# A hybrid pooling and attention block on one Trainium2 core: pooling's running sums moved from DMAs to VectorE, attention's halves added in DRAM while the attention still runs

## The chip, the cores and the metric

The kernel runs on one core of one Trainium2 chip, in one launch. The metric is the device time of that launch in microseconds (us); smaller is better. The core has TensorE (PE) for matrix products, VectorE (DVE), ScalarE (ACT), GpSimd (POOL) and SyncE (SP). SP, ACT and POOL can each put DMAs on their queue; DMAs that add to their destination are issued by POOL in this kernel. Everything is float32. Products run in "float32r" with each operand split into a high part and a low remainder, and three passes (high by high, high by low, low by high) are added.

## The reference, cut to what matters

One decoder layer on x of 1024 positions by 1024 channels:

```python
h = rmsnorm(x, g_mix_pre)
u_pool, q, k, v, gates = split(h @ w_in + b_in)
# pooling: 4 groups of 128 channels, windows 2, 4, 8, 16 along the sequence
pooled[g][t] = (cs[t] - cs[t - w]) / min(t + 1, w)          # a running mean, cs = cumsum(u_pool)
y_pool = ((pooled - u_pool) @ w_pool[g]) * pool_scale
# attention: 8 query heads on 2 key/value heads, window 128, with a sink logit per head
y_attn = softmax_with_sink(rotary(q) @ rotary(k).T) @ v
merged = sigmoid(gate_p) * (y_pool @ w_branch_pool) + sigmoid(gate_a) * (y_attn @ w_branch_attn)
x = x + rmsnorm(merged @ w_out, g_mix_post)
x = x + rmsnorm(square(relu(rmsnorm(x) @ w_up)) @ w_down, g_mlp_post)
```

A window that is a power of two can be summed by doubling: a sum over 2 is t[i] + t[i-1], a sum over 4 is that result plus itself shifted by 2, and so on. Windows 2, 4, 8 and 16 take 1, 2, 3 and 4 such steps, ten in all.

## The kernel before, in words

Activations lie with channels on the 128 partitions and the 1024 positions in the free dimension, except in the attention, where positions lie on partitions. Products with large weights (gates and pooling input, output projection, up and down projection) use a seven-product scheme: the class `Pairs` (L471) takes weight tiles in pairs and needs the products 1 to 7 of each pair, `gt.mm(bank, p, i)` at L544 being one of them (12 matmuls). Pairs 0 to 7 give the 16 gate tiles, pairs 8 and 9 the four pooling input tiles (numbers 16 to 19, one per pooling group).

In time, the parts that matter here follow each other like this.

1. **Attention** (to about 165 us). For each of the 8 query blocks n, `attend_v` (L419 to L432) multiplies probabilities by values. Because of how the two key/value heads are laid on the partitions, its result `yt` holds both heads, each in two halves of the softmax sum that still have to be added: one on partitions 0 to 63, one on 64 to 127. ACT copies the PSUM bank `yb` to `yt` (L430) and SP stores all of it to DRAM (`y_dram`, 8 tiles, L431). `yt` comes from the pool `yy`, which has four buffers and also gives `tf` of blocks 2, 3 and 7, `wpt`, a raw weight tile, and later the gate results. PE, DVE and ACT follow an order written out by hand; SP's and POOL's are left to the scheduler. In between, `fill` feeds PE with products of the gate stage.
2. **A first gate part** (165 to 210 us), in which PE, DVE, ACT and SP are ordered by hand. x is read again (`load_x`), scaled (`scale_gate`, L817), combined (`sum_gate`, L822 to L825) and split into the operands T1 to T4 (`split_gate`).
3. **The loop over p = 1 to 6** (L1074 on). Each turn does, for PE, products 6 of pair p, 4 and 3 of pair p-1, 5 and 7 of pair p: 60 matmuls. DVE adds the bank of the fifth product to a result (L1084) before PE may go on with product 3 in the same bank, prepares the next pair's weights (`sums56`, `sums37`, `split56`, `split37`), and multiplies by the row norms (L1094, L1101). ACT does copies out of PSUM, the high halves of the splits, sigmoids and the stores of finished gates to `z_dram`. The four pooling input tiles are finished between the start of the loop and turn p = 3 and kept in `chains`: `chain_start(gi)` adds the bias on ACT and stores the tile to `u_dram` through ACT's queue. `chain_steps` then does the doubling with DMAs on POOL's queue: for the first step it adds the tile in `u_dram`, shifted, to the tile in SBUF (L758); for each further step it first stores the tile to `s_dram` (L754) and then adds that back, shifted. The order is in `STEPS`, turns 2 to 6, with one last step after the loop.
4. **After the loop** (292 to 316 us) pair 7 is finished. `attn_load` (L1033 on, called in turn p = 6) has read the attention's result: for each of four tiles, SP reads one half in two DMAs of 64 partitions, and POOL adds the other half in two adding DMAs (both L1039), 16 DMAs in all. `attn_hi` (ACT, L1044) and `attn_lo` (DVE, L1049) split it.
5. **Branch products** (316 to 409 us). For m = 0 to 7 `mm_fm` (L455, L457) multiplies the attention result by `w_branch_attn`, 24 matmuls each, in two of four "mm" banks; `ba_mul(m - 1)` (DVE, L1134) multiplies the banks by the gate, which frees them for m + 1. Interleaved in DVE's order are `pool_diff` (L771 to L773, the running sum over w minus u) and `pool_split`. `pool_load` reads u back from `u_dram` into a `yy` buffer (L766). Then eight more products with the pooling branch.
6. Output projection, up projection, and from 797 us the down projection. In the last, `operands` (L1764) loads each step's two tiles; raw tiles come from a pool `dl` that lies where the up projection's buffers were.

The order of DVE's and ACT's work is fixed by the program, so an instruction that waits holds everything behind it on its engine.

Of the kernel before, what the change touches and what calls it, by code (L numbers as in the profile page):

```python
# [14 lines left out]
P = 128  # L15
# [35 lines left out]
def block_kernel(ctx: ExitStack, tc, xt, x, consts, vecs, sinks, b_qkv, g_post, g_mlp, g_mlp_post,  # L51
# [13 lines left out]
    z_dram, y_dram, u_dram, s_dram = (spill[i:j] for i, j in ((0, 16), (16, 24), (24, 28), (28, 32)))  # L65
    cnt = [0]

    def nm(s):
        cnt[0] += 1
        return f"{s}_{cnt[0]}"  # L70
# [16 lines left out]
    def bank(tag, shape=None):  # L87
        return psum["pool"].tile([P] + (shape or [512]), F32, tag=tag, name=nm(tag), bufs=psum["bufs"][tag])
# [330 lines left out]
    def attend_v(n):  # L419
        pt, pc = probs.pop(n)  # L420
        yt = yy.tile([P, 2, 512], F32, tag="y", name=nm("yt"))
        vp = ((vs[n - 1], pt), (dvs[n], pc)) if n else ((vs[0], pt),)
        yb = bank("sc", [2, 512])

        mms = [(kv, v, p, ph) for v, p in vp for ph in range(2) for kv in range(2)]
        for j, (kv, v, p, ph) in enumerate(mms):
            c = WINDOW[kv][ph]
            pe.matmul(yb[:, kv], v[:, c:c + P], p[ph][:, 4 * kv:4 * kv + 4].rearrange("p i q -> p (i q)"),  # L428
                      start=j < 2, stop=j >= len(mms) - 2)
        act.copy(flat(yt), flat(yb))  # L430
        nc.sync.dma_start(y_dram[:, :, n * P:(n + 1) * P].rearrange("c p q -> p c q"),  # L431
                          flat(yt).rearrange("p (c q) -> p c q", q=P))  # L432


    rb = bcp.tile([P, 1024], F32, tag="bc", name="rb_all")

# [305 lines left out]
    def chain_start(gi):  # L742

        f = chains[gi][0]
        act.activation(f, f, AF.Identity, bias=vec[:, V_BU + gi:V_BU + gi + 1])
        nc.scalar.dma_start(u_dram[gi], f)
        chains[gi] = f, 1

    def chain_steps(gis):

        for gi in gis:
            f, step = chains[gi]
            if step > 1:
                nc.gpsimd.dma_start(s_dram[gi], f)  # L754
        for gi in gis:
            f, step = chains[gi]
            src = (u_dram if step == 1 else s_dram)[gi]
            nc.gpsimd.dma_start(f[:, step:], src[:, :S - step], accum_op=ALU.add)  # L758
            chains[gi] = f, 2 * step

    pool_raw = {}

# [76 lines left out]
    with tc.manual_schedule(engines={mybir.EngineType.PE, mybir.EngineType.DVE, mybir.EngineType.Activation}):  # L839
# [39 lines left out]
        for n in range(NT):  # L879
# [38 lines left out]
                gt.load(17, yy.tile([P, NK, P], F32, tag="y", name="r17"))  # L918
            if n + 2 < NT:
                softmax_max(n + 2)  # L920
        gt.sums56(8)
        gt.sums37(8)
        fill(1e3)
# [1 line left out]
        flush(between[1])  # L925
        gt.operand(7, 2)
        gt.load(18)
    ap_pool.__exit__(None, None, None)
    psa_pool.__exit__(None, None, None)
    psum["pool"] = ctx.enter_context(tc.tile_pool(name="ps", bufs=4, space=bass.MemoryType.PSUM,  # L930
# [30 lines left out]
    with tc.manual_schedule(engines={mybir.EngineType.PE, mybir.EngineType.DVE, mybir.EngineType.Activation,  # L961
# [3 lines left out]
        load_x(2, g_place)  # L965
        gt.m1(6, bank("mm"), ga_.tile([P, S], F32, tag="ga", name=nm("f0")))
        gt.split37(8, wslot)
        gt.m1(7, bank("mm"), ga_.tile([P, S], F32, tag="ga", name=nm("f0")))
        gt.split56(8, wslot)
        gt.sums56(9)  # L970
        gt.sums37(9)
        for p in (6, 7):
            gt.m2(p)
            nc.sync.dma_start(f_spill(p), gt.f0.pop(p))
            if p == 6:
                gt.split37(9, ar)
# [55 lines left out]

    def attn_load(th, kh):  # L1033
        t = attn_raw[th, kh] = xp.tile([P, 2, 512], F32R, tag="x", name=nm("yalo"))
        for i, q in enumerate((nc.sync, nc.gpsimd)):
            for kv in range(2):
                src = y_dram[4 * kv + 2 * kh:4 * kv + 2 * kh + 2, :, th * 512:(th + 1) * 512]
                r = (kv + i) % 2 * HD
                q.dma_start(f32(t)[kv * HD:(kv + 1) * HD], src[:, r:r + HD].rearrange("m p q -> p m q"),  # L1039
                            **({"accum_op": ALU.add} if i else {}))  # L1040

    def attn_hi(th, kh):
        hi, lo = xp.tile([P, 2, 512], F32R, tag="x", name=nm("yahi")), attn_raw[th, kh]
# [14 lines left out]
    with tc.manual_schedule(engines=MANUAL):  # L1058
# [705 lines left out]
    def operands(i, s_):  # L1764
# [275 lines left out]
```

## Time and profile before

| | |
|---|---|
| three runs | 1107.94, 1113.25, 1116.89 us (median 1113.25) |
| the profiled execution | 1112.14 us, of which the span is 1110.4 us |
| PE busy in the span | 1093.3 us (98%) |
| DVE, ACT, POOL busy | 783.1, 593.6, 80.6 us |
| DMA | 226.78 MB moved, mean 204 GB/s |
| instructions | 13853, 5090 of them matmuls |

How to read it: the span is the time from the first to the last instruction of one profiled execution; the execution's own time is 1.7 us longer. Busy times of engines overlap, so they don't add up to the span. A row of the timeline gives start, duration, engine, line of the kernel, operation, output and inputs; the bracket at its end gives how long the engine had been idle before it and what ended that. A row of the windows gives, for a stretch of the span, the busy time of each engine, then the TensorE clock that was granted (1.00 is full speed) and the share of the 16 DMA engines that was busy. `yalo` is the attention result, `z` and `g` are gate or pooling tiles, `d` is the pooling input read back.

### The profile page before, as it was taken

The page shows a single profiled execution, that of the slowest core. Times are in us where ns is not written, and L with a number is a line of the kernel's source. Part 1 is how long each engine was busy: PE and PEld are TensorE (multiplying, and loading weights), DVE is VectorE, ACT ScalarE, POOL GpSimd, SP SyncE. Part 2 cuts the span into 40 slices and gives each one's busy share as a digit, 9 for nine tenths or more (in the row PEclk, how much of TensorE's full clock was granted, in tenths as well). Part 3 has the DMA queues.
Part 4 walks back from the last instruction along what each step waited for, and adds up shares of the span by engine and source line. Part 5 has one row for each costly group of instructions (what it writes and reads, how often), then busy time and mean ns, then how long its engine had stood idle before and what let it go on. Part 6 is the DMA issues. An engine that isn't in the chain of part 4 may idle for free.

```text
span 1110.4 us, 13853 instructions
## 1 busy us (share of the span) xinstructions
PE 1093.3 (98%) x5090; PEld 905.1 (82%) x5090; DVE 783.1 (71%) x1074; ACT 593.6 (53%) x976; POOL 80.6 (7%) x144
## 2 busy tenths in 40 slices
PE   9999999999988999999999999999999999999997
PEld 8888887888876888888888888888878888888886
DVE  6578897987565687988966756565546875447797
ACT  7558875465331137666755645455446535435462
POOL 0333100111310001200000000000000000000000
PEclk9999999999999999999999999999999999999999
DMA  9616689699998557922455543435698875332652
GB/s 342 166 39 210 202 252 330 200 314 324 288 275 288 165 165 152 292 100 102 167 186 205 196 177 141 172 124 210 220 337 296 298 271 195 102 98 69 226 180 94
DMA packets 96853, 226.78 MB, mean 204 GB/s; under 512 B 10001, under 2 KB 22929, under 8 KB 96785
## 3 DMA queue, kind: packets, MB, share of 16 engines
q1 hardware_dynamic: 82224, 183.04, 48.2%
q0 software_dynamic: 8512, 22.01, 9.3%
q10 hardware_dynamic: 6048, 20.84, 4.8%
q8 instruction: 40, 0.66, 0.2%
q14 instruction: 29, 0.23, 0.1%
HBM read 161.89 MB, written 62.92 MB: 202 GB/s over the span
## 4 chain that ended last, share of the span: by engine, by line
PE 85%; DVE 4%; issue 4%; DMA 3%; ACT 3%; POOL 1%; DVEq 0%; SPq 0%; POOLq 0%; ACTq 0%
PE mm L544 24%; PE at L544 17%; PE mm L1808 11%; PE at L1808 10%; PE mm L1343 5%; PE mm L455 3%; PE mm L192 2%; PE sc L183 2%; PE mm L183 2%; PE at L1343 2%; PE mm L457 2%; PE sc L428 1%; PE sc L360 1%; DVE wh L104 1%; PE at L1389 1%
## 5 line engine op out<-in xcount | busy, mean ns | idle before, releaser
L1808 PE MATMUL at<-ar,wh 128*128 128x512 f32 x696 | 159.3, 389 | 0.6 <-ACT ar L101 0.6
L1808 PEld LDWEIGHTS at<-ar,wh 128*128 128x128 f32 x696 | 130.5, 188 | 28.5 <-ACT ar L101 1.0
L1808 PE MATMUL mm<-ar,wh 128*128 128x512 f32 x576 | 131.0, 389 | 0.0
L1808 PEld LDWEIGHTS mm<-ar,wh 128*128 128x128 f32 x576 | 108.1, 188 | 22.5
L104 DVE TENSOR_TENSOR wh<-raw,wh 128x1024 fp32r<-128x1024 f32 x51 | 62.4, 1223 | 78.9 <-ACT wh L101 78.8
L101 ACT CAST wh<-raw 128x1024 fp32r<-128x1024 f32 x51 | 53.7, 1053 | 113.9 <-PE at L1808 50.8
L104 DVE TENSOR_TENSOR wh<-st,wh 128x512 fp32r<-128x512 f32 (+1 forms) x101 | 74.6, 746 | 32.4 <-ACT wh L101 27.9
L101 ACT CAST wh<-st 128x512 fp32r<-128x512 f32 (+1 forms) x100 | 65.2, 658 | 48.4 <-PE mm L455 25.7
L544 PE MATMUL mm<-T,wx 128*128 128x512 f32 x372 | 89.5, 389 | 0.0
L544 PEld LDWEIGHTS mm<-T,wx 128*128 128x128 f32 x372 | 69.8, 188 | 14.5
L544 PE MATMUL mm<-gr,wh 128*128 128x512 f32 x321 | 78.4, 395 | 1.3 <-DVE gr L104 1.3
L544 PEld LDWEIGHTS mm<-gr,wh 128*128 128x128 f32 x321 | 60.6, 190 | 14.3 <-DVE gr L104 1.6
L544 PE MATMUL mm<-T,wh 128*128 128x512 f32 x267 | 66.8, 392 | 3.1 <-DVE z L1165 3.1
L544 PEld LDWEIGHTS mm<-T,wh 128*128 128x128 f32 x267 | 50.4, 189 | 13.9 <-issue 3.5
L544 PE MATMUL at<-gr,wh 128*128 128x512 f32 x243 | 59.0, 389 | 0.0
L544 PE MATMUL mm<-x,wh 128*128 128x512 f32 x240 | 58.9, 394 | 0.0
L544 PEld LDWEIGHTS at<-gr,wh 128*128 128x128 f32 x243 | 45.6, 188 | 9.5
L544 PE MATMUL at<-T,wx 128*128 128x512 f32 x213 | 52.0, 389 | 0.0
L544 PEld LDWEIGHTS mm<-x,wh 128*128 128x128 f32 x240 | 44.2, 188 | 9.6 <-ACT f L653 0.2
L544 PEld LDWEIGHTS at<-T,wx 128*128 128x128 f32 x213 | 40.0, 188 | 8.3
L104 DVE TENSOR_TENSOR ar<-B,ar 128x1024 fp32r<-128x1024 f32 x37 | 45.1, 1220 | 2.0 <-ACT ar L101 1.5
L544 PE MATMUL at<-ar,wh 128*128 128x512 f32 x192 | 46.1, 389 | 0.0
(468 smaller groups left out, 2112.4 us busy)
## 6 DMA issues: line engine op xcount, KB each, us to landing
raw<-f_dram SPq DMA_DIRECT2D x53, 512.0 KB, 3.8
f_dram<-g SPq DMA_DIRECT2D x28, 512.0 KB, 3.0
st<-in_w_up_dram SPq DMA_DIRECT2D x24, 512.0 KB, 5.5
B<-in_w_dn_dram SPq DMA_DIRECT2D x24, 512.0 KB, 7.3
g<-spill_dram SPq DMA_DIRECT2D x19, 512.0 KB, 6.1
f_dram<-g ACTq DMA_DIRECT2D x17, 512.0 KB, 2.8
st<-in_w_g_dram SPq DMA_DIRECT2D x16, 512.0 KB, 5.7
raw<-in_w_dn_dram SPq DMA_DIRECT2D x16, 512.0 KB, 4.8
```

Source lines behind the costliest of these rows:

```text
L101: act.copy(hi, src)
L104: eng.tensor_tensor(lo, src, f32(hi), ALU.subtract)
L183: pe.matmul(bq, xs_[k][n // 4][:, xh, n % 4 * P:(n % 4 + 1) * P], wq[k][:, h, :], start=k == 0 and j == 0, stop=k == NK - 1 and j == 2)
L192: pe.matmul(bkv_of(n), xs_[k][n // 4][:, xh, n % 4 * P:(n % 4 + 1) * P], wkv[k // 2][:, h, k % 2, :], start=k == 0 and j == 0 and not (joi ...
L360: pe.matmul(sb[:, kv, i, :nk], qt[r, qx, m * P:(m + 1) * P], kx[r, k0:k0 + nk], start=j == 0, stop=j == 2)
L428: pe.matmul(yb[:, kv], v[:, c:c + P], p[ph][:, 4 * kv:4 * kv + 4].rearrange("p i q -> p (i q)"), start=j < 2, stop=j >= len(mms) - 2)
L455: pe.matmul(bs[th], whi[:, k, :], rhs(k, hl, th), start=k == 0 and hl == 0, stop=False)
L457: pe.matmul(bs[th], wlo[:, k, :], rhs(k, 0, th), start=False, stop=k == nk - 1)
L544: pe.matmul(b, w[wh][:, kt, :], x_, start=not after and kt == 0 and j == 0, stop=kt == 3 and j == 2, skip_group_check=after)
L1343: pe.matmul(bs[t], Am[a][k][ah][:, t * P:(t + 1) * P], Wm[w][k][wh], start=not after and k == 0 and j == 0, stop=k == 3 and j == 2, skip_g ...
L1389: pe.transpose(b[:, i, :], hs[4 * th + i][:, k * P:(k + 1) * P], ident)
L1808: pe.matmul(bs[t], fo[fh][:, k2, t * P:(t + 1) * P], wo_[wh][:, k2, :], start=not after and s2 == 0 and k2 == 0 and j == 0, stop=(s2, k2) ...
```

## The change

Five things change.

- The attention's halves: `y_dram` has four tiles instead of eight. After `attend_v(n)`, SP stores two halves of `yt` (64 partitions each, 256 KB) instead of one 512 KB tile. Behind the next block, `attend_sum(n - 1)` issues two adding DMAs on POOL's queue that add the other halves into the same place in DRAM; `yt` is kept until then. `attn_load` is four plain SP DMAs of 128 partitions, and is called in turn p = 5 instead of 6.
- The running sums: each of the ten steps is one DVE addition of the tile to itself shifted, into a new tile, and a DVE copy of its first `step` columns. The new tiles come from the pools `gp` (groups 0 and 2), `ga` or `yy` (groups 1 and 3). `STEPS` is a new order, in turns 3 to 6 with the last step after the loop. The tile for `u_dram` is stored through SP's queue instead of ACT's.
- In the first gate part, `split56(8)` stands before product 1 of pair 7, `scale_gate(1)` stands earlier, and `sum_gate(1)` stands before `split56(9)`.
- In the down projection, one raw tile (product 1, step 3) comes from the pool `st` instead of `dl`.
- The spill tensor has 24 tiles instead of 32.

```diff
-        nc.sync.dma_start(y_dram[:, :, n * P:(n + 1) * P].rearrange("c p q -> p c q"),
-                          flat(yt).rearrange("p (c q) -> p c q", q=P))
+        for kv in range(2):
+            attend_store(nc.sync, n, yt, kv, kv)
+        halves[n] = yt
+    def attend_store(q, n, yt, kv, h, **how):
+        q.dma_start(y_dram[:, kv * HD:(kv + 1) * HD, n * P:(n + 1) * P].rearrange("m p q -> p m q"),
+                    yt[h * HD:(h + 1) * HD, kv, :].rearrange("p (m q) -> p m q", q=P), **how)
+    def attend_sum(n):
+        yt = halves.pop(n)
+        for kv in range(2):
+            attend_store(nc.gpsimd, n, yt, kv, 1 - kv, accum_op=ALU.add)
...
-        nc.scalar.dma_start(u_dram[gi], f)
+        nc.sync.dma_start(u_dram[gi], f)
...
         for gi in gis:
             f, step = chains[gi]
-            if step > 1:
-                nc.gpsimd.dma_start(s_dram[gi], f)
-        for gi in gis:
-            f, step = chains[gi]
-            src = (u_dram if step == 1 else s_dram)[gi]
-            nc.gpsimd.dma_start(f[:, step:], src[:, :S - step], accum_op=ALU.add)
-            chains[gi] = f, 2 * step
+            if gi % 2 == 0:
+                t = g32([S])
+            elif 2 * step < WINDOWS[gi]:
+                t = ga_.tile([P, S], F32, tag="ga", name=nm("t"))
+            else:
+                t = gate_result()
+            dve.tensor_tensor(t[:, step:], f[:, step:], f[:, :S - step], ALU.add)
+            dve.tensor_copy(t[:, :step], f[:, :step])
+            chains[gi] = t, 2 * step
...
+            if n:
+                attend_sum(n - 1)
...
         gt.split37(8, wslot)
+        gt.split56(8, wslot)
         gt.m1(7, bank("mm"), ga_.tile([P, S], F32, tag="ga", name=nm("f0")))
-        gt.split56(8, wslot)
...
             if p == 6:
                 gt.split37(9, ar)
+                scale_gate(1)
+        gt.operand(8, 4)
+        sum_gate(1)
         gt.split56(9, ar)
-        gt.operand(8, 4)
-        scale_gate(1)
...
         gt.mm(b3[8], 8, 3)
-        sum_gate(1)
...
-        for i, q in enumerate((nc.sync, nc.gpsimd)):
-            for kv in range(2):
-                src = y_dram[4 * kv + 2 * kh:4 * kv + 2 * kh + 2, :, th * 512:(th + 1) * 512]
-                r = (kv + i) % 2 * HD
-                q.dma_start(f32(t)[kv * HD:(kv + 1) * HD], src[:, r:r + HD].rearrange("m p q -> p m q"),
-                            **({"accum_op": ALU.add} if i else {}))
+        nc.sync.dma_start(f32(t), y_dram[2 * kh:2 * kh + 2, :, th * 512:(th + 1) * 512].rearrange("m p q -> p m q"))
...
-    STARTS, STEPS = {1: 1, 2: 3, 3: 0, 4: 2}, {2: (1,), 3: (1, 3), 4: (3, 0), 5: (3, 2), 6: (3, 2)}
+    STARTS, STEPS = {1: 1, 2: 3, 3: 0, 4: 2}, {3: (1, 1), 4: (0, 3), 5: (3, 3, 3), 6: (2, 2)}
...
-            if p == 6:
+            if p == 5:
                 for o in ORDER:
                     attn_load(*o)
...
-            ft = raw_tile()
+            ft = stage([2, 512]) if (i, s_) == (1, 3) else raw_tile()
```

More of the change, by code (lines that the diff above doesn't have):

```diff
@@ L63, in block_kernel @@
     psum = {"pool": psa_pool.__enter__(), "bufs": {"sc": 2, "mm": 4}}
-    z_dram, y_dram, u_dram, s_dram = (spill[i:j] for i, j in ((0, 16), (16, 24), (24, 28), (28, 32)))
+    z_dram, y_dram, u_dram = (spill[i:j] for i, j in ((0, 16), (16, 20), (20, 24)))
     cnt = [0]
@@ L430, in attend_v @@
         act.copy(flat(yt), flat(yb))
-        nc.sync.dma_start(y_dram[:, :, n * P:(n + 1) * P].rearrange("c p q -> p c q"),
-                          flat(yt).rearrange("p (c q) -> p c q", q=P))
+        for kv in range(2):
+            attend_store(nc.sync, n, yt, kv, kv)
+        halves[n] = yt
+    halves = {}
+    def attend_store(q, n, yt, kv, h, **how):
[5 more added lines that the diff above has]
+            attend_store(nc.gpsimd, n, yt, kv, 1 - kv, accum_op=ALU.add)
     rb = bcp.tile([P, 1024], F32, tag="bc", name="rb_all")
@@ L927, in block_kernel @@
         gt.load(18)
+        attend_sum(NT - 1)
     ap_pool.__exit__(None, None, None)
@@ L2031 @@
     x1 = nc.dram_tensor("x1_dram", (NT, P, D), F32, kind="Internal").ap()
-    spill = nc.dram_tensor("spill_dram", (32, P, S), F32, kind="Internal").ap()
+    spill = nc.dram_tensor("spill_dram", (24, P, S), F32, kind="Internal").ap()
     wbp = nc.dram_tensor("wbp_dram", (8, P, 4, P), F32, kind="Internal").ap()
```

## The prediction

> **What bounds the kernel now.** I read the page first, for the busy shares; then PE's waits; then the windows around those waits, for their length and the clock behind them; then POOL's, ACT's and DVE's timelines, for what was late.
>
> ```profile
> span 1110.4 us, 13853 instructions
> PE 1093.3 (98%) x5090; PEld 905.1 (82%) x5090; DVE 783.1 (71%) x1074; ACT 593.6 (53%) x976; POOL 80.6 (7%) x144
> ...
> PE mm L455 <- DVE g L1134: 3.1, 2, 2.1
> PE mm L544 <- DVE z L1165: 3.1, 1, 3.1
> PE mm L544 <- DVE gr L104: 1.3, 1, 1.3
> ...
> PE at L1808 <- ACT ar L101: 0.6, 1, 0.6
> ```
>
> PE is busy for 1093.3 of 1110.4 us and the change removes no matmul. So it can win only in PE's 17.1 us of idle time and in time lost to a lower clock. The four rows (us in total, times, longest) hold 8.1 us of that. By the timeline they lie at 306 to 352 us (the first two rows), at 184 us and at 813 us.
>
> ```profile
> 305.80:308.90 3.10, 0.03 (x1) 0.03 (x1) 2.57 (x4) 2.15 (x3) 2.02 (x3) 0.97 1.09 210
> 308.90:315.97 7.07, 7.07 (x24) 5.72 (x25) 2.82 (x3) 1.50 (x3) 0.11 (x1) 0.77 1.02 303
> 337.90:339.20 1.30, 0.27 (x3) 0.06 (x1) 1.27 (x5) 0.75 (x1) 0.00 (x0) 1.00 1.00 407
> 350.30:352.50 2.20, 0.10 (x1) 0.02 (x1) 2.17 (x5) 0.70 (x1) 0.00 (x0) 1.00 0.65 257
> 352.50:358.10 5.60, 5.59 (x17) 4.35 (x18) 3.40 (x5) 0.34 (x1) 0.00 (x0) 0.70 0.59 205
> ...
> 237.80:251.40 13.60, 13.60 (x62) 11.26 (x61) 13.21 (x16) 8.75 (x11) 2.62 (x3) 1.00 1.04 313
> 251.40:265.00 13.60, 13.60 (x62) 11.27 (x61) 9.76 (x12) 8.03 (x10) 0.58 (x2) 1.00 1.04 376
> 265.00:278.60 13.60, 13.60 (x62) 11.27 (x61) 9.38 (x11) 7.08 (x9) 2.28 (x3) 1.00 1.04 280
> 278.60:292.20 13.60, 13.60 (x62) 11.27 (x61) 9.29 (x11) 6.49 (x8) 3.72 (x4) 1.00 1.02 275
> ```
>
> After the length, the columns are PE, PEld, DVE, ACT, POOL, the granted clock, DMA share and GB/s. The last four rows are turns p = 3 to 6 of the loop, at full clock: 13.60 us for 60 matmuls, 0.227 us each. Stall A is 3.08 us long and the clock is 0.77 behind it: 24 matmuls take 7.07 us instead of 5.44, another 1.63 us. Stall B (1.03 us) keeps the clock at 1.00. Stall C (2.11 us) is followed by 0.70: 23% to 30% off for about 5.6 us, 0.30 x 5.60 = 1.7 us. The three cost 3.08 + 1.63 + 1.03 + 2.11 + 1.7 = 9.55 us.
>
> [...]
>
> ```profile
> 306.88 0.96 POOL L1039 DMA_DIRECT2D yalo<-spill_dram  x1 [1.42 <-issue]
> 334.32 0.57 POOL L754 DMA_DIRECT2D spill_dram<-g  x1 [11.10 <-DMA g<-spill_dram]
> 340.56 0.85 POOL L758 DMA_DIRECT2D g<-spill_dram  x1 [5.67 <-DMA spill_dram<-g]
> ...
> 300.65 1.05 ACT L1044 CAST yahi<-yalo 128x1024 fp32r<-128x1024 f32 x1 [7.28 <-DMA yalo<-spill_dram]
> 315.96 1.05 ACT L1044 CAST yahi<-yalo 128x1024 fp32r<-128x1024 f32 x1 [5.11 <-DMA yalo<-spill_dram]
> ...
> 308.08 0.68 DVE L1165 TENSOR_TENSOR z<-f,mm 128x512 f32<-128x512 f32 x1
> 320.02 1.22 DVE L1175 TENSOR_TENSOR z<-z,rb_all 128x1024 f32<-128x1024 f32 x1
> 336.93 1.23 DVE L771 SCALAR_TENSOR_TENSOR d<-g,d 128x1023 f32<-128x1023 f32 x1 [6.22 <-DMA d<-spill_dram]
> 350.26 1.22 DVE L771 SCALAR_TENSOR_TENSOR d<-g,d 128x1017 f32<-128x1017 f32 x1 [4.27 <-issue]
> ```
>
> The common cause is POOL's queue. A store waits for the add before it and an add for the store, 5.67 and 11.10 us in these rows; the adds of the attention (L1039) are queued among them and end at 307 us. So ACT waits for `yalo`, twice, and holds the copies and sigmoids behind it; DVE reaches L1165 only at 308.08 (stall A). The last sigmoid's product (L1175) comes at 320.02, its buffer is free late, and the pooling input that takes it arrives at 336.93 (stall B, in front of `ba_mul`). The last add, issued at 340.56, gives DVE its tile at 350.26 (stall C).
>
> **The change part by part.** *Adds of the attention.* ACT finds all of `yalo` in SBUF, so its waits of 7.28 and 5.11 us go. L1165 then needs its bank, which PE finishes at about 303 (turn 6 ends at 292.2, and four products of 12 matmuls, 2.72 us each, follow), and DVE's work behind the loop: five instructions of 0.68 us and four of 1.2 to 1.3 us, one of them a running sum, 8.3 us from 292.2 on and so done in time. PE wants L1165 at 305.8, 2 us later. Stall A: -4.71. What is late next is gate 15: L1175 stands behind the fourth `attn_lo`, which waited for the tile of 315.96; without that it follows PE's product in its bank (305.8 + 2.72) and about 2.5 us of DVE work, at 311 instead of 320.0. So the pooling input lands some 9 us earlier, near 328, while PE wants that `ba_mul` near 333. Stall B: -1.03, covered by 5 us. *Running sums off POOL's queue.* The last one is done by DVE near 294, so stall C goes: -3.8. ACT loses four store issues; SP takes them, and its `attn_load` issues fall from eight to four; no row of PE's waits names a load in this loop, so zero. POOL loses all issues of L754 and L758 and eight of L1039, and what is left behind them there only comes earlier. An `attn_load` one turn earlier waits at worst for weight buffers freed at the end of turn 4 (265.0); behind it on SP stand pair 7's loads, wanted in turn 6 (from 278.6): zero, with 13.6 us of cover.
>
> *What DVE gains in work.* A step is an addition like L1094, whose successor starts 1.13 us later, and a small copy like L772.
>
> ```profile
> 218.77 1.22 DVE L1094 TENSOR_TENSOR z<-z,rb_all 128x1024 f32<-128x1024 f32 x1
> 219.90 0.68 DVE L104 TENSOR_TENSOR wh<-g,wh 128x512 fp32r<-128x512 f32 x1
> 338.07 0.15 DVE L772 TENSOR_TENSOR g<-g,cst 128x1 f32<-128x1 f32 x1
> ...
> 240.50 0.68 DVE L1084 TENSOR_TENSOR z<-z,at 128x512 f32<-128x512 f32 x1
> 252.08 0.69 DVE L1084 TENSOR_TENSOR z<-z,at 128x512 f32<-128x512 f32 x1 [0.21 <-ACT z L1083]
> 257.31 1.22 DVE L104 TENSOR_TENSOR wx<-ws,wx 128x1024 fp32r<-128x1024 f32 x1 [1.88 <-ACT wx L101]
> 265.68 0.69 DVE L1084 TENSOR_TENSOR z<-z,at 128x512 f32<-128x512 f32 x1 [2.12 <-ACT z L1083]
> 279.28 0.69 DVE L1084 TENSOR_TENSOR z<-z,at 128x512 f32<-128x512 f32 x1 [2.98 <-ACT z L1083]
> ...
> 243.27 5.44 PE at L544 x24
> ```
>
> One step is 1.13 + 0.15 = 1.28 us: 2.56 in turns 3, 4 and 6, 3.84 in turn 5, 1.28 behind the loop, 12.8 in all. They stand ahead of L1084, and PE's product 3 waits for L1084. In turn 3 L1084 ends at 241.18 and PE wants it at 243.27 (chain row; then every 13.60 us): a lead of 2.09 us. Less 2.56 that is a stall of 0.47. From there to turn 4 DVE's own row is 11.58 us long with 0.43 idle; 11.15 + 2.56 = 13.71 against 13.60, a stall of 0.11. Turn 4 to 5: 13.60 less 4.2 idle (1.88, 2.12 and one of 0.21) plus 3.84 is 13.2: lead 0.4. Turn 5 to 6 has 4.1 idle and 2.56 of steps: lead 1.9. That is 0.6 us if DVE can fill all its idle time; where it hands a tile to ACT and back it can't, and I allow 0.4 more: +1.0. The ends: 0 if the loads of turn 2 land earlier on less busy DMA engines and raise the lead; 12.8 if no idle time can be filled.
>
> *Adds during the attention.*
>
> ```profile
> yalo<-spill_dram SPq DMA_DIRECT2D x8, 256.0 KB, 11.7
> yalo<-spill_dram POOLq DMA_DIRECT2D x8, 256.0 KB, 8.0
> ...
> st<-in_w_ba_dram SPq DMA_DIRECT2D x8, 256.0 KB, 6.6
> ...
> 90.00:165.00 75.00, 74.58 (x419) 61.14 (x418) 67.23 (x93) 61.56 (x159) 11.50 (x20) 1.00 0.70 223
> ...
> 99.05 0.79 POOL L330 TENSOR_TENSOR df<-vf,vf 128x128 f32<-128x128 f32 x1
> ...
> 109.52 1.02 ACT L430 COPY yt<-sc 128x1024 f32<-128x1024 f32 x1
> ```
>
> POOL is busy for 11.50 of 75 us here; sixteen issues of 0.96 us are 15.4 more, and the pieces of v behind them are wanted two or three blocks later: zero. SP issues eight stores more: zero. What counts is the buffer `yt`, kept until its add has landed. The tight place is block 3, whose `yt` at 109.52 needs the one of block 1: POOL is free at 99.84, issues until 101.8, and with 8.0 us to landing is done at 109.8, 0.3 us late. The 8.0 were measured with DMA share above 1.0 and here it is 0.70, so I take 0; the long end is the row of 11.7, 4 us late, on ACT, which is 82% busy here.
>
> [...]
>
> *The first gate part and the raw tile.*
>
> ```profile
> 178.34 1.23 DVE L104 TENSOR_TENSOR ar<-ws,ar 128x1024 fp32r<-128x1024 f32 x1 [2.07 <-DMA spill_dram<-f]
> ```
>
> DVE waits 2.07 us there in `split56(9)` while `sum_gate(1)` stands behind it; moved ahead, it fills that gap, and PE's wait of 1.3 us for `gr` goes: -1.3 (ends: 0, if x lands late because its `yy` buffers are still held by adds, and -1.3). For the raw tile, the wait of 0.6 us for `ar` at 813 goes only if the raw tile's partner is early too: -0.3 (ends 0 and -0.6).
>
> Sum: -4.71 - 1.03 - 3.8 + 1.0 + 0 - 1.3 - 0.3 = -10.1. The profiled execution took 1112.14 us, so 1102.0. It lies 1.1 us under the median of the three runs, 1113.25; against the median the forecast is 1103.
>
> **The rivals.** *Half the gain.* One of stalls A and B stays because something else is late: gate 15's buffer, or `attn_load`. For it: both hang on loads, and the 11.7 us of `yalo` on SP are the longest landing shown. Against it: 5 and 13.6 us of cover. Price: A back is +4.7, so 1108. [...] *The attention holds its buffer.* The adds land later than 8 us, ACT waits at L430, and the banks of the scores are late. With 4 us in two or three blocks: +8 to +12, so 1111 to 1115. Against it: DMA share 0.70 there, above 1.0 where the 8.0 and 11.7 were measured. *DVE becomes the bound: slower than before.* Place: L1084 in turns 3 to 6. It decides when DVE's idle time (0.4, 4.2, 4.1 us between the turns) is mostly hand-over to ACT that can't be filled, or a new tile has to wait for a buffer whose gate is still being stored. Then 12.8 us come back in four pieces over 2 us, with a slow clock of 1.7 us behind three: 1112 - 11.1 + 12.8 + 5 = 1119. For it: with the steps DVE is at 53 of 54.4 us over the four turns. Against it: its waits of 1.88 to 2.98 us are for PE's own progress, which is lead and not loss.
>
> **How the numbers follow.** Forecast 0.55 (1098 to 1107), half the gain 0.12, the clock rule 0.05, the attention 0.10, DVE 0.18. About 1% is what a measurement of this kernel can tell from no change: 1102.1 and 1124.4. Of the forecast's 0.55 just under half ends below 1102.1, faster 0.27. DVE's case ends above 1124 only if other waits follow, 0.10; the attention's in 0.03; with some allowance for the orders of SP and POOL, which the scheduler makes anew, slower 0.16. Same 0.57. The range, 1097 to 1118, takes in all of these but the worse half of DVE's case, and a margin of 1 us below the forecast's own.
>
> **What would show it.** Right: no wait for L1165 or L1134 in PE's waits, clock 1.00 from 300 to 360 us, no L758 on POOL, L1084's idle before it near zero in turns 4 and 5. Wrong: PE waits for L1084 over 1 us each, ACT idle before L430, or PE idle near 184 us.

## The result and the profile after

The changed kernel takes 1101.51 us (median of 6 runs, 1100.77 to 1104.17) against 1112.8 us for the kernel before (median of 6, 1107.94 to 1116.89): a ratio of 0.990, 95% interval 0.988 to 0.993. The forecast was 1103.0 us. The profiled execution took 1100.77 us, of which 1098.8 us are the span; before it was 1112.14 and 1110.4.

The page of the changed kernel and all of PE's waits from 0.3 us on (us in total, times, longest), then windows over the place of the three stalls:

```profile
span 1098.8 us, 13865 instructions
PE 1088.6 (99%) x5090; PEld 903.2 (82%) x5090; DVE 794.8 (72%) x1094; ACT 593.8 (54%) x976; POOL 75.2 (7%) x136
...
PE mm L201 <- DVE pad L160: 1.1, 1, 1.1
PE at L555 <- DVE ar L104: 0.5, 1, 0.5
PE at L555 <- ACT ar L101: 0.3, 1, 0.3
PE sc L360 <- ACT yt L430: 0.3, 1, 0.3
...
300.00:320.00 20.00, 20.00 (x90) 16.57 (x89) 15.49 (x20) 9.32 (x11) 0.00 (x0) 1.00 0.73 243
320.00:340.00 20.00, 20.00 (x89) 16.54 (x89) 15.01 (x25) 6.31 (x8) 0.00 (x0) 1.00 0.76 270
340.00:360.00 20.00, 20.00 (x90) 16.56 (x89) 6.32 (x11) 1.55 (x3) 2.43 (x2) 1.00 0.58 143
```

The waits for L1165 and L1134 (now L1176 and L1145) are gone, and so is the one for `gr`. Through the place of stalls A, B and C PE is busy for all of 60 us at full clock. Of the two small waits for `ar`, the one of 0.3 us is new and the one of 0.5 us has grown from 0.2.

To see where each microsecond went, I cut both spans at the same work: the start of the run of 36 matmuls that stands at 207.91 us in the chain of before (from there to the next cut: "the loop"), the start of the matmuls of L1343, of the down projection, and of its second product. Windows of the kernel before, then of the changed kernel (length, then PE, PEld, DVE, ACT and POOL busy, clock, DMA share, GB/s):

```profile
0.00:207.91 207.91, 204.99 (x1157) 171.49 (x1158) 161.40 (x247) 142.21 (x321) 39.62 (x96) 1.00 0.68 220
207.91:408.89 200.98, 194.76 (x841) 159.53 (x841) 140.45 (x183) 77.11 (x98) 25.84 (x30) 0.98 0.85 259
796.67:841.58 44.91, 44.27 (x194) 36.04 (x193) 25.92 (x24) 19.53 (x22) 0.00 (x0) 1.00 0.87 318
```

```profile
0.00:207.79 207.79, 205.26 (x1157) 171.29 (x1158) 160.60 (x247) 141.79 (x321) 54.17 (x112) 1.00 0.77 220
207.79:398.19 190.40, 190.40 (x842) 157.66 (x841) 152.27 (x203) 76.67 (x98) 6.48 (x7) 1.00 0.67 219
786.14:830.11 43.97, 43.82 (x193) 35.96 (x193) 25.91 (x24) 19.37 (x22) 0.00 (x0) 1.00 0.89 325
```

The loop gained 200.98 - 190.40 = 10.58 us and holds no idle time now: 190.40 of 190.40 us. The stretch ahead of it gained 0.12 and the first down product 0.78 us: the last window shown for the kernel before begins 0.16 us too early in the work (its first matmul starts at 796.67 us, that of the changed kernel at 785.98 and not at 786.14), so at the same work it is 44.75 against 43.97. The other stretches differ by at most 0.1 us. So the whole gain of 11.6 us is the loop and 0.8 us of the down projection. Of the 10.58, 200.98 - 194.76 = 6.22 were idle, and in 194.76 - 190.40 = 4.36 PE was busy for longer with the same matmuls. Behind stall A (308.70 to 312.11 us) and behind stall C (353.07 to 356.49) the clock was 0.50, which is worth up to 3.4 of these 4.36; the rest was lost at full clock.

### The profile page after: what moved, and what is told of

Its sections match the earlier page's. It is cut to its first block, busy times and chain, and to the rows that moved or that the text cites. A ratio compares the mean times of both kernels' runs of the same rounds, so it can differ in the third digit from the quotient of the medians.

```text
span 1098.8 us, 13865 instructions
## 1 busy us (share of the span) xinstructions
PE 1088.6 (99%) x5090; PEld 903.2 (82%) x5090; DVE 794.8 (72%) x1094; ACT 593.8 (54%) x976; POOL 75.2 (7%) x136
## 4 chain that ended last, share of the span: by engine, by line
PE 92%; DMA 3%; DVE 2%; ACT 1%; issue 1%; SPq 0%; POOL 0%; DVEq 0%; ACTq 0%; POOLq 0%
PE mm L555 24%; PE at L555 18%; PE at L1819 14%; PE mm L1819 12%; PE mm L466 5%; PE mm L1354 5%; PE mm L468 3%; PE mm L183 2%; PE at L1354 2%; PE mm L192 2%; PE sc L183 2%; DMA spill_dram<-yt 1%; PE sc L428 1%; PE sc L360 1%; PE at L1400 1%
```

## The experiments

The line numbers of each kernel differ by a few. "Start" is the start of the loop, "loop" its length, both from the same cut as above; a group (rows 3 to 6, 7 to 10, 11 to 14) shares one chip and the runs of the kernel before, and the ratio is to these.

| run | start | loop | median us (range) | ratio, 95% |
|---|---|---|---|---|
| before | 207.91 | 200.98 | | |
| after | 207.79 | 190.40 | 1101.51 | 0.990 [0.988, 0.993] |
| sums only | 206.42 | 190.82 | 1101.22 (1101.05 to 1101.66) | 0.9915 [0.9893, 0.9938] |
| attention only | 209.55 | 190.40 | 1104.81 (1104.22 to 1105.7) | 0.9948 [0.9928, 0.9967] |
| old orders | 212.00 | 190.40 | 1104.28 (1102.67 to 1107.06) | 0.9937 [0.9911, 0.9964] |
| old raw tile | 207.36 | 190.40 | 1101.74 (1100.91 to 1104.54) | 0.9924 [0.9901, 0.9946] |
| after again | 207.68 | 190.40 | 1102.82 (1102.14 to 1103.1) | 0.9894 [0.987, 0.9918] |
| sums, orders, raw tile | 205.60 | 191.46 | 1099.71 (1099.05 to 1100.62) | 0.9867 [0.9844, 0.9891] |
| after, DMA setting doubled | 205.96 | 190.40 | 1100.95 (1099.49 to 1101.08) | 0.9878 [0.9851, 0.9906] |
| after, rows of 2 KB | 205.78 | 190.41 | 1099.76 (1099.04 to 1101.5) | 0.987 [0.9845, 0.9895] |
| before, DMA setting doubled | 206.89 | 195.92 | 1108.08 (1103.3 to 1113.05) | 0.9957 [0.9931, 0.9982] |
| after, each sum twice | 208.51 | 198.70 | 1110.38 (1108.68 to 1112.63) | 0.9986 [0.9969, 1.0004] |
| after with stalls | 207.69 | 203.91 | 1114.52, one run | |
| before, attention early | 206.30 | 202.45 | 1113.48, one run | |

The changed kernel was profiled twice; the two spans are 1098.8 and 1101.1 us, and 1.6 us of the difference are waits of 0.8 us in the output projection and 0.8 us at the end. So one profile's span can't show a difference of 2 us; lengths of a stretch and the waits in it can, and the loop of the changed kernel was 190.40 us both times.

**Which half removes which stall?** Two kernels have one half each, both with the old orders and the old raw tile. Sums only is the kernel before with the running sums on VectorE, the new `STEPS` and the store of `u_dram` on SP's queue:

```diff
-            if step > 1:
-                nc.gpsimd.dma_start(s_dram[gi], f)
...
-            nc.gpsimd.dma_start(f[:, step:], src[:, :S - step], accum_op=ALU.add)
+            dve.tensor_tensor(t[:, step:], f[:, step:], f[:, :S - step], ALU.add)
+            dve.tensor_copy(t[:, :step], f[:, :step])
```

Attention only is the kernel before with the halves added in DRAM and read once, in turn 5:

```diff
+    def attend_sum(n):
+        yt = halves.pop(n)
+        for kv in range(2):
+            attend_store(nc.gpsimd, n, yt, kv, 1 - kv, accum_op=ALU.add)
```

> The kernel before with only the running sums on VectorE in the new order (u stored through SyncE); the attention halves are still added by POOL at the read, the first gate part and the raw tile are as before. Theory (POOL's queue as a whole is the cause): stall C goes because no sum is on the queue, and A and B go too because the eight adds of the attention start when their tiles are read instead of behind the sums; the three are 9.55 us, so about -9 us, ratio 0.992. Rival (the adds themselves are slow and late): A and B stay, only C goes, -3.9 us, ratio 0.9965. If VectorE were the bound instead, waits for L1084 of over 1 us in turns 3 to 6 and a ratio above 1.

> The kernel before with only the attention halves added in DRAM during the attention and one plain read; the running sums still go through POOL's DMAs in the old order, first gate part and raw tile as before. Theory (POOL's queue as a whole): A and B go because nothing has to be added at the read, and the sums move up by the 23 us that the eight adds took on the queue (284 to 307), so C goes too: about -9 us, ratio 0.992. Rival (each stall has its own cause): C stays, -5.7 us, ratio 0.995.

The loop's windows, of sums only and of attention only:

```profile
206.42:397.24 190.82, 190.69 (x841) 157.57 (x841) 152.61 (x203) 76.89 (x98) 13.64 (x14) 1.00 0.74 229
```

```profile
209.55:399.95 190.40, 190.40 (x841) 157.66 (x841) 140.52 (x183) 76.97 (x98) 18.19 (x22) 1.00 0.82 263
```

Either half alone removes all three stalls. With the sums on VectorE, the attention's adds still go through POOL's queue, but the last is issued at 290.7 us instead of 306.88. With the attention's adds gone, the running sums still go through it, but the last is issued at 318.8 instead of 340.56. The gains don't add: the two halves fix the same thing. The ratio of attention only is the one expected for a stall C that stays, but C is not there: the loop has all of its gain. In its profile the losses lie elsewhere, 1.64 us ahead of the loop, which starts at 209.55 us, and 1.2 us behind the first down product. The next groups show what happens ahead of the loop.

**The orders and the raw tile.** Each is undone in the changed kernel, first the orders:

```diff
-        gt.split56(8, wslot)
         gt.m1(7, bank("mm"), ga_.tile([P, S], F32, tag="ga", name=nm("f0")))
+        gt.split56(8, wslot)
...
-                scale_gate(1)
-        gt.operand(8, 4)
-        sum_gate(1)
         gt.split56(9, ar)
+        gt.operand(8, 4)
+        scale_gate(1)
...
+        sum_gate(1)
```

Then the raw tile:

```diff
-            ft = stage([2, 512]) if (i, s_) == (1, 3) else raw_tile()
+            ft = raw_tile()
```

> The changed kernel with the old order in the first gate part (split56(8), split56(9), scale_gate(1), sum_gate(1)). The changed kernel gained only 0.1 us up to 208 us where 1.3 was forecast. Theory: the adds of the attention hold the buffers of x, so x comes 2 to 6 us later, which costs about what the new order gains; with the old order PE's waits between 165 and 208 us are 1 to 2 us longer than in the changed kernel: ratio to before 0.991 to 0.993. Rival: the order is worth nothing, the time is that of the changed kernel within 0.3 us in the trace.

> The changed kernel with the raw tile of product 1, step 3 from the old pool. The changed kernel gained 0.94 us between the first down product and 45 us later, where 0.3 was forecast. Theory: all of that is the buffer, so the stretch is 44.9 us long again instead of 43.97 and the time rises by 0.9 us. Rival: the early loads came earlier for another reason, and the stretch stays at 44.0.

With the old orders PE waits 1.2 us for `gr` again, as before; in both profiles of the changed kernel that wait is absent. Its ratio is a little worse than expected. Its start at 212.00 us is later than that wait explains: PE also waited 1.6 us for `yt` in the attention, and the clock from 100 to 160 us was 0.97, as much as a clock of 0.50 for 3 to 4 us would give. This wait comes and goes: it is 0.3 us in most profiles, 0.8, 1.2 and 1.6 in one each. With the old raw tile the first down product takes 44.56 us instead of 43.97: 0.59 us.

**Why did the stretch ahead of the loop gain so little?** In the changed kernel, the chain of waits (start, us, what) runs through the attention's adds into the load of x; then PE's rows there:

```profile
150.59 5.65 DMA spill_dram<-yt
...
156.89 1.02 POOL spill_dram L438
157.91 5.14 issue
163.05 5.21 DMA spill_dram<-yt
...
168.82 6.27 DMA xr<-in_xt_dram
...
176.21 0.73 PE L555 MATMUL at<-x,ar 128*128 128x512 f32 x2 [0.34 <-ACT ar L101]
177.47 2.56 PE L555 MATMUL at<-x,ar 128*128 128x512 f32 x10 [0.53 <-DVE ar L104]
```

The add issued at 163.05 lands at 168.26, and only then can x be loaded into the buffer that its `yt` held; the work on x keeps ACT and DVE from `ar`. The telling line is "5.14 issue": POOL has issued the first add of block 6 and waits 5.14 us before the second, for nothing that the profile shows. POOL's waits sum this up:

```profile
POOL spill_dram L438 <- issue: 40.7, 8, 8.8
```

All eight pairs have such a gap. An add has 256 pieces of 512 bytes. My suspects, which no view names, were this number and a setting of the program for its DMAs, `dynamic_dma_scratch_size`. Four kernels on one chip test them: the changed kernel again, one without the attention's half, one with the setting doubled, and one with 64 pieces of 2 KB per add.

Sums, orders, raw tile is the changed kernel with the attention's store, loads and turn of the kernel before:

```diff
-        for kv in range(2):
-            attend_store(nc.sync, n, yt, kv, kv)
-        halves[n] = yt
+        nc.sync.dma_start(y_dram[:, :, n * P:(n + 1) * P].rearrange("c p q -> p c q"),
+                          flat(yt).rearrange("p (c q) -> p c q", q=P))
...
-            if p == 5:
+            if p == 6:
```

The setting doubled is one number:

```diff
-    nc = bacc.Bacc("TRN2", target_bir_lowering=False, num_devices=1, dynamic_dma_scratch_size=1024)
+    nc = bacc.Bacc("TRN2", target_bir_lowering=False, num_devices=1, dynamic_dma_scratch_size=2048)
```

Rows of 2 KB is another layout of `y_dram`, with each load cut in two to match:

```diff
+    y_blocks = y_dram.rearrange("m p q -> (m p q)").rearrange("(n p m q) -> n p m q", n=NT, p=P, m=4)
-        q.dma_start(y_dram[:, kv * HD:(kv + 1) * HD, n * P:(n + 1) * P].rearrange("m p q -> p m q"),
+        q.dma_start(y_blocks[n, kv * HD:(kv + 1) * HD],
```

> The changed kernel as it is, beside the kernels of this group. Both theories: span 1098.8 us as in its profile, the first gate part with waits for ar of 0.5 and 0.3 us, about 1101 us, ratio to the kernel before 0.990 to 0.993.

> The running sums on VectorE, the new order of the first gate part and the moved buffer, with the attention halves added on the way into SBUF as in the kernel before. Theory (the DRAM adds hold the yy buffers into which x is loaded, and so eat what the new order gains): without them x lands early and nothing waits near 176 to 186 us; the shared part of the loop starts at 206.4 us (the profile of sums alone starts it 1.0 us earlier than the changed kernel and still waits 0.36 us for gr), and the loop has no wait for L1165's bank as with sums alone. Span 206.4 + 190.6 + 388.0 + 44.0 + 174.1 + 94.6 = 1097.7, 1.1 us under the changed kernel. Rival (the two edits of the attention are worth something in the loop once the rest is in): the loop is longer than 191 us, span over 1099.

> [...] Rival (the second add waits for its own half's store or for the first add's transfer): the distances stay at 3.7 to 9.9 us, span 1098.8.

> The changed kernel with another layout of the attention's result in DRAM: by block, so that each row of a half store or add is 2048 bytes in one piece instead of four of 512; the loads in the loop are cut in two DMAs each. [...] Rival (the transfer sets the distance): the distance shrinks only as far as the landing does, and at equal landing stays at 3.7 to 9.9 us; span 1098.8.

With the setting doubled, POOL's last pair, and PE at the place of the two waits:

```profile
165.95 2.07 POOL L438 DMA_DIRECT2D spill_dram<-yt  x2 [8.34 <-ACT f L563]
...
175.88 2.88 PE L555 MATMUL at<-x,ar 128*128 128x512 f32 x12
```

Both adds of a pair go out in 2.07 us, x is loaded at 165.50 and 178.46 instead of 167.35 and 182.16, and PE runs its twelve matmuls without a break. The loop starts 1.7 us earlier than in the changed kernel of the same group; with rows of 2 KB, 1.9 us; without the attention's half, 2.1 us. So the distance between the adds of a pair hangs on the setting and on the number of pieces, not on the landing: the two issues of a pair took 2.06 to 2.30 us in all with the setting doubled and 1.65 to 1.89 us with 64 pieces, while the adds landed after 5.7 and 5.3 us (medians), no sooner than the 4.8 us of the changed kernel of this group. That the adds held the buffers of x was borne out in all three. In the kernel without the attention's half a rival was half right as well: its loop is 191.46 us, over the 191 named, with a wait of 0.6 us for ACT (L1145) that the changed kernel doesn't have. On this chip each of the twelve times of these three kernels (at most 1101.5 us) is below all four of the changed kernel (at least 1102.14). So the two at 1099.7 and 1099.8 us are better than both kernels, by 0.3% against the changed one. For the attention's half this means that, with the setting at 1024, it cost more than it gave once the sums were on VectorE: without it the median is 3.1 us lower.

**Is POOL's queue late for the same reason in the kernel before?** The gaps between the adds in front of 307 us look alike. If they hang on the setting too (the theory called space below), they go when it is doubled. The kernel before is run with the same doubled number:

```diff
-    nc = bacc.Bacc("TRN2", target_bir_lowering=False, num_devices=1, dynamic_dma_scratch_size=1024)
+    nc = bacc.Bacc("TRN2", target_bir_lowering=False, num_devices=1, dynamic_dma_scratch_size=2048)
```

And, by itself, with the attention's loads and adds one turn earlier:

```diff
-            if p == 6:
+            if p == 5:
                 for o in ORDER:
                     attn_load(*o)
```

> [...] Theory (space): the gaps of 1.2 to 4.2 us between the eight adds of the attention in front of 307 us go, since no row of before names work they wait for. The last is issued near 292 instead of 306.88 us, ACT has its tiles when it asks, and the two running sums behind them land some 14 us earlier: no PE wait for L1165, L1134's waits gone, loop 190.4 to 192 us instead of 200.98; about 9 us under the kernel before, ratio 0.992. Rival (the chain of stores and adds, which wait for each other's landing, makes POOL's queue late): the adds may move up, but stall C stays and A shrinks at most by half; loop over 195 us, ratio 0.996 or more.

> The kernel before with its loads and adds of the attention's result issued one turn earlier (in turn 5 instead of turn 6) and nothing else. Theory (POOL's queue as a whole is late, by as much as its issues and gaps add up to): the adds are done some 14 us earlier and stall A goes, but the running sums of turns 5 and 6 stand behind them and come later, so that stall C, 2.1 us before, grows by several us; span 1108 to 1118. Rival (only the place of the adds in the queue was wrong): A and C both go, span about 1101.

The kernel before with the setting doubled: POOL's queue, ACT's first copy, the landing of POOL's adds and PE behind stall A:

```profile
283.37 6.59 POOL L1039 DMA_DIRECT2D yalo<-spill_dram  x6
...
300.20 1.05 ACT L1044 CAST yahi<-yalo 128x1024 fp32r<-128x1024 f32 x1 [7.36 <-DMA yalo<-spill_dram]
...
yalo<-spill_dram POOLq DMA_DIRECT2D x8, 256.0 KB, 16.5
...
308.46:312.50 4.04, 4.04 (x11) 3.21 (x12) 2.81 (x3) 2.96 (x4) 0.00 (x0) 0.58 1.03 406
```

Half of each theory. Six of the eight adds go out without a gap (gaps of 3.87 and 2.90 us are left), and what stood behind them comes earlier (the last running sum at 333.51 instead of 340.56): stalls B and C are gone, the loop is 5.06 us shorter. But A stays, 3.16 us: issued early, the adds land after 16.5 us instead of 8.0 (medians). The DMA engines are full in both kernels, with a share of 1.03 from 280 to 300 us here and of 1.02 there before, and the adds that were issued earlier stayed in flight for longer. ACT has its first tile at 300.20, before at 300.65. So the gaps in the queue made B and C; they did not make A.

The kernel before with the attention one turn earlier, one run: ACT's first copy, the last running sum, and PE:

```profile
294.33 1.05 ACT L1044 CAST yahi<-yalo 128x1024 fp32r<-128x1024 f32 x1
...
344.26 0.85 POOL L758 DMA_DIRECT2D g<-spill_dram  x1 [6.79 <-DMA spill_dram<-g]
...
352.13 0.76 PE L455 MATMUL mm<-yahi,wh 128*128 128x512 f32 x1 [8.32 <-DVE g L1134]
```

A is gone and C has grown from 2.11 to 8.32 us, as the queue theory had it: the adds moved forward pushed the last running sum back, from 340.56 to 344.26 us. (A wait of 1.2 us for ACT, L1083, is new in this loop.)

**Is VectorE's lead what the prediction said?** Each running sum's addition is done twice, into the same tile, so that the output stays as it is.

```diff
-            dve.tensor_tensor(t[:, step:], f[:, step:], f[:, :S - step], ALU.add)
+            for _ in range(2):
+                dve.tensor_tensor(t[:, step:], f[:, step:], f[:, :S - step], ALU.add)
```

> The changed kernel with the addition of every running sum done twice into the same tile, 1.13 us more per step. Theory (VectorE's work stands in front of the tile that PE wants, and its lead is 1.1, 1.05, 1.4 and 3.0 us in turns 3 to 6): PE waits for at L1095's successor 1.2, 2.3, 3.0 and 0.7 us in turns 3 to 6, 7.2 us together, and two of these stalls are followed by a slow clock as in the kernel before, 1.7 us each: span 1098.8 + 10.6 = 1109, ratio about 1.000. Rival (VectorE's idle stretches elsewhere in the turn can be filled): at most 3 us in all, span under 1102.

PE's rows with a wait in turns 3 to 5, then windows of the second and the third wait and of the work behind each:

```profile
244.48 3.06 PE L555 MATMUL at<-x,wh 128*128 128x512 f32 x12 [0.62 <-DVE z L1096]
260.67 3.02 PE L555 MATMUL at<-x,wh 128*128 128x512 f32 x12 [2.25 <-DVE z L1096]
277.72 4.37 PE L555 MATMUL at<-x,wh 128*128 128x512 f32 x12 [3.16 <-DVE z L1096]
...
258.40:260.67 2.27, 0.02 (x1) 0.00 (x1) 2.24 (x5) 0.00 (x0) 0.00 (x0) 1.00 0.85 290
260.67:264.20 3.53, 3.53 (x15) 2.92 (x16) 3.46 (x5) 2.22 (x4) 0.00 (x0) 1.00 0.97 346
274.50:277.72 3.22, 0.07 (x1) 0.00 (x0) 3.15 (x5) 0.00 (x0) 0.00 (x0) 0.92 0.45 163
277.72:282.00 4.28, 4.28 (x13) 3.45 (x14) 4.21 (x6) 2.54 (x4) 0.00 (x0) 0.66 0.00 0
```

The waits are 0.62, 2.25, 3.16 and 0 where 1.2, 2.3, 3.0 and 0.7 were expected: lead less added work gives the stall, to 0.7 us. The clock slowed behind one of them, not two. The loop is 8.30 us longer (6.03 idle, 192.67 - 190.40 = 2.27 slow) against 10.6 expected; that the span of 1109.4 us still fits the expected 1109 is luck, since 0.7 us lie ahead of the loop and 1.6 in the last stretch.

**How long may PE idle at full clock?** Extra VectorE work, which leaves its tiles as they are, in front of three `ba_mul`.

```diff
+            for _ in range({3: 6, 5: 7, 7: 11}.get(m, 0)):
+                dve.tensor_tensor(ba_gate[m - 1], ba_gate[m - 1], ba_gate[m - 1], ALU.max)
```

> The changed kernel with idempotent VectorE instructions put in front of the three ba_mul of m = 3, 5 and 7 (6, 7 and 11 of them), so that PE stalls by about 1.7, 2.8 and 4.2 us with 100% work between. Theory (as the kernel before shows: idle times of 2.1 and 3.1 us are each followed by some 1.6 us lost to slow matmuls, one of 1.0 us by none): the stall of 2.8 and that of 4.2 us lose 1.6 us each, the one of 1.7 us less than 1. [...]

```profile
334.53 0.47 PE L466 MATMUL mm<-yahi,wh 128*128 128x512 f32 x1 [1.73 <-DVE g L1145]
352.10 0.77 PE L466 MATMUL mm<-yahi,wh 128*128 128x512 f32 x1 [6.36 <-DVE g L1145]
...
352.10:358.00 5.90, 5.90 (x14) 4.62 (x15) 5.83 (x8) 0.00 (x0) 1.22 (x1) 0.52 0.65 134
```

The stalls came out as 1.73, 6.36 and two of under 1 us, not as planned, so this run doesn't test 2.8 us. The one of 1.73 us lost no clock, the one of 6.36 did. The clock rows of the profiles say more, though. In the kernel before the clock is 0.50 from 308.70 to 312.11 us and from 353.07 to 356.49 us, two intervals of 3.41 us that begin 13 such steps apart. I laid steps of 3.41 us over the other profiles too, from where their clock falls (with each sum twice at 277.2 us, by the rows of 0.92 and 0.66 above). On these steps, the interval with stall C and the one behind it in the kernel before, then the two intervals that the stall of 2.25 us touches in the kernel with each sum twice:

```profile
349.66:353.07 3.41, 1.30 (x7) 0.63 (x5) 2.77 (x6) 1.05 (x1) 0.00 (x0) 1.00 0.61 244
353.07:356.49 3.42, 3.42 (x9) 2.73 (x9) 2.83 (x4) 0.00 (x0) 0.00 (x0) 0.50 0.55 196
...
256.75:260.16 3.41, 1.67 (x8) 1.05 (x6) 3.38 (x6) 0.63 (x1) 0.00 (x0) 1.00 1.02 382
260.16:263.57 3.41, 2.90 (x13) 2.40 (x14) 3.34 (x6) 1.59 (x3) 0.00 (x0) 1.00 0.89 324
```

Stall C lies whole in one interval, which is idle for 2.11 of 3.41 us (62%), and the next runs at half clock. The stall of 2.25 us is cut by a step into 1.74 us (51%) and 0.51 us, and no interval runs slow. The stall of 1.73 us is cut in the same way, into 1.05 and 0.68 us, and the clock is 1.00 from 334.53 to 338.00 us.

## Why the prediction came out

The time was right to 1.5 us, and the place of the gain was right: the three stalls and the slow matmuls behind them. That it came so close is in part luck: the loop gave 1.0 us more than forecast, VectorE's work cost 1.0 less and the down projection gave 0.5 more, while the first gate part gave 1.2 less. By its steps:

- *Stalls A, B and C, -9.55.* They are gone; the loop gained 10.58. The idle part was exact (3.08 + 1.03 + 2.11 = 6.22). The clock's part was right too: 3.3 forecast, and two stretches of 3.41 us at a clock of 0.50 are worth up to 3.4. What the prediction has no term for is the other 1.0 us or so of the 4.36, lost at full clock: single matmuls near the stalls and near 319 us that take 0.30 to 0.34 us from start to start instead of 0.23, and the last one before each stall, which counts with its whole 0.39 us because no other starts behind it.
- *"The common cause is POOL's queue", with A put down to the attention's adds and C to the running sums.* The cause was right as a whole and the division wrong. Either half alone removes all three, so the two terms are not a sum. The total came out only because each stall was counted once. And A is not the queue's gaps: with these gone it stood at 3.16 us, since the adds, issued earlier, then took 16.5 us to land. It goes when the adds start earlier, or when either half takes its transfers off.
- *VectorE's lead, +1.0.* It was 0. These are VectorE's rows of the changed kernel ahead of PE's product in turns 3 to 6, and PE's chain rows (start, us):

```profile
238.81 1.22 DVE L770 TENSOR_TENSOR t<-z 128x1023 f32<-128x1023 f32 x1
239.95 0.15 DVE L771 COPY t<-z 128x1 f32<-128x1 f32 x1
...
241.34 0.68 DVE L1095 TENSOR_TENSOR z<-z,at 128x512 f32<-128x512 f32 x1
255.02 0.68 DVE L1095 TENSOR_TENSOR z<-z,at 128x512 f32<-128x512 f32 x1
268.30 0.68 DVE L1095 TENSOR_TENSOR z<-z,at 128x512 f32<-128x512 f32 x1
280.26 0.68 DVE L1095 TENSOR_TENSOR z<-z,at 128x512 f32<-128x512 f32 x1
...
243.15 5.44 PE at L555 x24
256.75 5.44 PE at L555 x24
270.35 5.44 PE at L555 x24
283.95 5.44 PE at L555 x24
```

  Ended 0.68 us after its start, L1095 leads by 1.1, 1.05, 1.4 and 3.0 us, and no row has idle time before it. The price of a step was right (1.13 + 0.15 us). What was missing is the lead: a weight load of turn 2, issued at 220.5 us in both kernels, landed 1.7 us earlier, and VectorE with it (228.11 instead of 229.81). Before, the add of a running sum went out just ahead of that load (L758, at 220.41 us), and it is gone; the DMA engines are full in both (share 0.97 and 0.99 while the load is under way), but move 297 instead of 256 GB/s. The prediction had named an earlier landing of turn 2's loads as the end at 0, and chose a value near it. The rival "DVE becomes the bound" was near all the same: with the additions doubled, its stalls are there and the gain is gone.
- *First gate part, -1.3.* The pair of profiles gives 0.12. The wait for `gr` went, as forecast. But the end at 0, "if x lands late because its `yy` buffers are still held by adds", happened too: waits for `ar` of 0.34 and 0.53 us (0.19 before) came in its place, with some slow matmuls. And the wait was not steady to begin with: it is 0.36 and 0.25 us instead of 1.25 in sums only and in before with the attention early, whose edits lie behind this stretch, and their loops start at 206.42 and 206.30 us. The loop of the changed kernel (two profiles) and of three variants with the same orders and adds starts at 207.36 to 208.51 us. So here the change as a whole gained nothing and may have lost 1 to 2 us: the adds cost more than the orders gave. Removing the adds' gaps brings the loop forward by 1.7 to 1.9 us, more than the whole term.
- *Adds during the attention, 0.* `yt` was held for no longer than PE could bear: 0.3 us of wait before and after. The step failed at the other end of the buffer. The prediction asked who needs `yt` next within the attention, and not who takes its buffer behind it; and it costed an add at its issue (0.96 us) and landing, not at POOL's wait between two issues, 40.7 us in all. Its landing of 8.0 us is that of adds of 256 KB; a half of `yt` is 128 KB and not 256 KB as said in the part on the change, and these adds landed after 5.0 us.
- *Raw tile, -0.3.* The buffer alone is worth 0.59 us (undone in the changed kernel), its better end. The pair of profiles shows 0.78 in that stretch; over all the profiles it takes 44.15 to 44.79 us with the old raw tile (six) and 43.52 to 44.08 with the new one (eight), so the rest is within what varies from profile to profile.
- *The clock rule, 0.05 of the chances.* No run shows a rule that this name could stand for. What the runs showed: the loop gained 10.58 us, more than the 6.22 that were idle, and behind the stalls of 3.08 and 2.11 us the clock was 0.50 for 3.41 us each. Length alone didn't tell which stalls cost clock, as the rows on the steps of 3.41 us show.

## What to carry to other kernels

When several stalls hang on one late queue, ask for each edit what is left of the queue, not which stall it names: terms that share a cause are alternatives, and the cheapest one may do it all. A buffer has an owner after the stage that fills it; follow it there before a hold is costed at zero. And read "issue" in the waits of a queue: here POOL stood for 40.7 us in front of eight adds, for nothing that the profile shows, and 64 pieces instead of 256 per add, or 2048 instead of 1024 in one setting, took that away.

## What the runs showed of the hardware

- The distance between two adds on POOL's queue. With `dynamic_dma_scratch_size=1024` and 256 pieces of 512 bytes per add, the second of a pair started 3.7 to 9.9 us after the first (the changed kernel). With 2048 it followed at once, and both issues of a pair took 2.06 to 2.30 us; with 64 pieces of 2 KB and 1024 it did so too, in 1.65 to 1.89 us. What POOL waits for in between, no view names.
- Idle stretches of PE and the clock behind them: 1.73 us (after with stalls) and 2.25 us (each sum twice) were followed by a clock of 1.00; 2.11 and 3.08 us (before) by one interval of 3.41 us at 0.50; 3.16 us by a clock of 0.58 over 4.04 us (before, setting doubled) and 0.66 over 4.28 us (each sum twice), about one such interval; 6.36 us (after with stalls) by 0.52 over 5.90 us, and 8.32 us (before, attention early) by 0.57 over 4.87 us, with 0.91 and 0.63 already over the stall itself, which makes about two and three of them. From start to start a slow matmul took 0.43 us instead of 0.23 (before, behind stall C). Since 2.11 us slowed the clock and 2.25 us did not, length alone doesn't tell them apart; the idle share of the interval between two steps of 3.41 us did. At full clock, the intervals that were idle for 84% and 62% (stalls A and C) were followed by half clock, and those idle for 51% (each sum twice) and about 52% (after with stalls, 344.09 to 347.50 us) were not. At half clock, one idle for about 35% (after with stalls, behind 350.9 us) was followed by another slow one, and those idle for 6% (behind stall A) and about 15% (each sum twice, behind 277.2 us) were not. One case doesn't fit: with the old orders, the wait of 1.6 us for `yt` in the attention, 47% of such an interval, came with a clock of 0.97 from 100 to 160 us. The matmuls around it are shorter than elsewhere (64 partitions, 256 columns, 277 ns instead of 389 in the changed kernel); whether that is why was not tested.
